# When conditioning tiles are loaded and multiplied in a hybrid decoder step: later loads, visits in pairs and triples, four tiles at the second norm

## The chip, the cores and the metric

One Trainium2 chip, one core. TensorE (PE) multiplies matrices into PSUM; VectorE (DVE), ScalarE (ACT) and GpSimd (POOL) do elementwise work; SyncE (SP) issues most of the DMA transfers from HBM into the on-chip SBUF. Each engine works through its own instructions in order, and engines wait for one another by semaphores. The metric is the device time of one execution in microseconds; a kernel's time is the median of its runs.

## The reference

One layer of a decoder, for a prompt (256 tokens) and eight samples of 4 tokens (288 token columns in all), D_MODEL 2048, float32:

```python
mod = jax.nn.silu(c) @ P['w_ada'] + P['b_ada']          # 9 conditioning rows, 2048 -> 6*2048
sh1, sc1, gt1, sh2, sc2, gt2 = [m[:, None, :] for m in jnp.split(mod, 6, axis=-1)]
xn = rmsnorm(x, P['g_norm1']) * (1.0 + sc1) + sh1
mix, st = mixer(xn, states[l], P)                       # RG-LRU, GLA and mLSTM branches, merged by gates
x = x + gt1 * mix
xn = rmsnorm(x, P['g_norm2']) * (1.0 + sc2) + sh2
x = x + gt2 * (jnp.square(jax.nn.relu(xn @ P['w_ff1'])) @ P['w_ff2'])
y = rmsnorm(x, g_final)
```

`mixer` multiplies `xn` by `w_in` (2048 x 12312), runs the three recurrent branches with their states, and merges them: `sum over branches of sigmoid(gate_b) * (y_b @ w_br_b)`, then `@ w_out`. All outputs, the new states too, are returned.

## The kernel before

**Layout.** Activations lie feature-major: 16 k-tiles of 128 features by 288 columns. SBUF holds ten large buffers (`slot(0)` to `slot(9)`, each 128 x 8 x 288), a ring buffer `ag` (one of 128 x 2048), two buffers `st` (128 x 1028; the states of GLA and mLSTM pass through them as well), and three buffers each for the weights' `raw`, `hi` and `lo`.

**Weight streams.** `stream` multiplies by a block of 512 output features. A step loads a 128 x 1024 weight tile (`raw`, L155, on SyncE's queue), rounds it to `hi` on ScalarE (L156), takes the rest `lo` on VectorE (L157), and does 24 matmuls of 288 columns: for four groups of features and two k-tiles hi x xh, hi x xl and lo x xh (L163 to L165). It yields after each step; `ahead` gives its loads and splits high priority.

**Conditioning.** `w_ada` is used by 16 k-rows for each of six vectors (SC1 in two halves of eight tiles, SH1, GT1, SH2, SC2, GT2 of sixteen tiles of 1024 KB each). `units()` lists them in the order in which they are needed, and after SH1 sixteen tiles of `win` for a correction (`cor`): the first three q/k/v blocks are multiplied before the shift SH1 is known, and SH1 times those weights is added at the end. `load_one` issues one tile's load (L264, L262 for `st`, where a tile is two halves, L270 for SC1, L276 for `cor`) into the next buffer of the list `slots["ids"]`; it waits in SyncE's queue until that buffer's earlier use is over. `visit` multiplies all loaded tiles on TensorE (L228) and, with the last of a vector, adds them up feature by feature (`by_feature` on VectorE, `ada_finish` or the correction's `finish`, L282 to L287). `drain(n)` loads and visits until n is done.

**Who comes when.** `every(p)` sets a pattern of letters, and `run` does one letter after each step of a stream: L loads a tile, V visits, X does both. `visit` is issued behind the last matmul of that step. SyncE is scheduled by hand, in the order of the program (`manual_schedule`); on the other engines a planner orders instructions by priority and by its own timeline.

**Stages.** SC1's first half is drained, `scale1(0)` scales k-tiles 0 to 7; three q/k/v blocks run over them (12 steps), then over k-tiles 8 to 15 (12 more), with pattern X. `shift` adds SH1: for four k-tiles at a time GpSimd adds xh + xl, VectorE and GpSimd add the shift, `split` makes new xh and xl. Then the fourth q/k/v block and two LRU blocks (24 steps, `cor`), the LRU, the gates, GLA, the merge of branch 0, the mLSTM with the merge of branch 1 filling in, the mLSTM's output gate `mo` (16 steps), the merge of branch 2 (48 steps; buffers 8 and 9 hold its input `yml`, buffer 5 the mLSTM's result `nT` before that), `wout` (32 steps), the second norm (`sumsq`, `rstd_of`, L1160 to L1166), and the MLP (`ff1`, `ff2`, 8 blocks).

Of the kernel before, what the change touches and what calls it, by code (L numbers as in the profile page):

```python
# [24 lines left out]
SH1, SC1, GT1, SH2, SC2, GT2 = range(6)  # L25
# [27 lines left out]
def trunk(ctx, tc, io):  # L53
    nc = tc.nc
    PSUM = bass.MemoryType.PSUM
    V, S, G, T, Q = nc.vector, nc.scalar, nc.gpsimd, nc.tensor, nc.sync
# [112 lines left out]
            yield  # L169


    pace = {"every": "", "n": 0, "last": None}

    def every(p):
        pace.update(every=p, n=0)

    def run(gen):
        for _ in gen:
            if pace["every"]:
                step(pace["every"][pace["n"] % len(pace["every"])])  # L180
                pace["n"] += 1


# [7 lines left out]
    mod = cp.tile([P, 6, KT, 9], F32, tag="mod", name="mod")  # L191
# [3 lines left out]
    def by_feature(ps, h, n):  # L195

        t = t288()[:, 0:n]
        V.transpose(t, ps[:, 256 * h:256 * h + n])
        return t.rearrange("p (m c) -> p m c", c=32)

    slots = {"ids": (None,), "n": 1}
# [11 lines left out]
    def cond_product(name, load, each, cols, stat, finish):  # L213


        acc_ = []

        def products(raw, q):
            if not acc_:
                acc_.append(pa.tile([P, 512], F32, tag="pa", name=nm("pa")))  # L220
            ps = acc_[0]
            w = cols // len(raw)
            for i in range(each):
                k = each * q + i
                for h, r in enumerate(raw):
                    v = r[:, w * i:w * i + w].rearrange("p (m j f) -> p j m f", j=4, f=32)
                    for j in range(4):
                        T.matmul(ps[32 * j:32 * j + 32, h * w // 4:(h + 1) * w // 4], stat(k), v[:, j], start=k == 0 and h == 0,  # L228
                                 stop=k == KT - 1, skip_group_check=True)

        def end():
            with tc.high_priority():
                for h in range(-(-cols // 1024)):
                    finish(h, by_feature(acc_[0], h, min(256, cols // 4 - 256 * h)))

        n = KT // each
        for q in range(n):
            def ld(q=q):
                raw = raw_tile()
                load(raw, q)  # L240
                return raw
            yield name, ld, lambda raw, q=q: products(raw, q), end if q == n - 1 else None
# [60 lines left out]
    def load_one():  # L303
        u = next(left, None)
        if u:
            held.append((u[0], u[1](), u[2], u[3]))

    def visit():

        while held:  # L310
            name, raw, products, end = held.pop(0)
            products(raw)
            if end:
                end()
                done.add(name)

    def step(c):
        if c in "LX":
            with tc.high_priority():
                load_one()  # L320
        if c in "VX":
            with tc.high_priority(), tc.issue_after(pace["last"].ins):
                visit()

    def drain(n):
        while n not in done:
            if not held:
                with tc.high_priority():
                    load_one()
            visit()  # L330


# [21 lines left out]
    def smp(a):  # L354
        return a[..., NP:N].rearrange("p k (b t) -> p k b t", b=NB)

    def modulate(xg, rs, k0, fk, xh, xl, xr):
# [3 lines left out]
        for j in range(0, 4, 2):  # L361
# [4 lines left out]
            G.tensor_tensor(out=xs, in0=xs, in1=mod[:, fk, r, 1:9].unsqueeze(3).to_broadcast(bc), op=ALU.mult)  # L366
            split(xh[:, r, :], xl[:, r, :], xr[:, j:j + 2])

    def shift(k0, shk, xh, xl, xr):

        h, l = xh[:, k0:k0 + 4, :], xl[:, k0:k0 + 4, :]
        G.tensor_tensor(out=xr, in0=h.bitcast(F32), in1=l.bitcast(F32), op=ALU.add)
        for i in range(4):
            V.tensor_scalar(xr[:, i, 0:NP], xr[:, i, 0:NP], mod[:, shk, k0 + i, 0:1], None, ALU.add)
        xs = smp(xr)
        G.tensor_tensor(out=xs, in0=xs, in1=mod[:, shk, k0:k0 + 4, 1:9].unsqueeze(3).to_broadcast([P, 4, NB, TS]), op=ALU.add)
        split(h, l, xr)

    def split(dst_h, dst_l, src):
        n = src.shape[1]  # L380
        step = 2 if len(src.shape) == 3 else n
        for a in range(0, n, step):
            r = slice(a, min(a + step, n))
            S.activation(dst_h[:, r], src[:, r], AF.Copy)  # L384
            V.tensor_tensor(out=dst_l[:, r], in0=src[:, r], in1=dst_h[:, r].bitcast(F32), op=ALU.subtract)  # L385
# [10 lines left out]
    xh = big.tile([P, KT, N], F32R, tag="xh", name="xh1")  # L396
# [24 lines left out]
    def plus_slot(dst, base):  # L421
        def f(m, p):
            V.tensor_tensor(out=dst[:, base + m, :], in0=dst[:, base + m, :], in1=p, op=ALU.add)
        return f
# [9 lines left out]
    scale1(0)  # L434
    G.tensor_copy(con[:, 0:1], mod[:, SC1, 0, 0:1])
    G.dma_start(con, io["con"])
    every("X")
    for b in range(NPRE):
        run(stream(win, B_Q + b, act1, 8, to_slot((qk, vv)[b // 2], 4 * (b % 2))))
    drain("sc")  # L440
    scale1(1)
    for b in range(NPRE):
        run(stream(win, B_Q + b, act1, KT, plus_slot((qk, vv)[b // 2], 4 * (b % 2)), k0=8))
    drain(SH1)
    for i in range(4):
        shift(4 * i, SH1, xh, xl, (xs3, xs4)[i % 2][:, 0:4, :])
    every("LLLL.V")
    slots.update(ids=(5, 6, 7, None, 0, 1, 3, 4), n=0)
    for b in range(NPRE, 4):
        run(stream(win, B_Q + b, act1, KT, to_slot((qk, vv)[b // 2], 4 * (b % 2))))  # L450
# [114 lines left out]
            V.scalar_tensor_tensor(sg[:, base + m, :], th, 1.0, p, ALU.add, ALU.mult)  # L565
        return f

    every("LLLL.V..")
    slots.update(ids=(6, 7, "st", None), n=0)
    run(stream(win, B_GATE, act1, KT, gate_silu(0)))  # L570
    run(stream(win, B_GATE + 1, act1, KT, gate_silu(4)))
# [225 lines left out]
    def merge(br, y, w):  # L797
        for b in range(4):
            if br == 0 and b == 2:
                visit()  # L800
                slots.update(ids=(None,), n=0)
                every("L.V...")
            if br == 0:
                gt = acc[b // 2][:, 4 * (b % 2):4 * (b % 2) + 4, :]
            elif br == 1:
                gt = ring.tile([P, 2048], F32, tag="ag", name=nm("ag"))[:, 0:4 * N].rearrange("p (k n) -> p k n", k=4)
            else:
                gt = slot(4)[:, 0:4, :]
            run(stream(win, B_MG + 4 * br + b, act1, KT, lambda m, p: S.activation(gt[:, m, :], p, AF.Tanh, scale=0.5)))

            def ev(m, p):
                k = 4 * b + m
                a = acc[k // 8][:, k % 8, :]
                if br == 0:
                    V.scalar_tensor_tensor(a, gt[:, m, :], 1.0, p, ALU.add, ALU.mult)
                    return
                t = t288()
                V.scalar_tensor_tensor(t, gt[:, m, :], 1.0, p, ALU.add, ALU.mult)  # L818
                G.tensor_tensor(out=a, in0=a, in1=t, op=ALU.add)  # L819
                if br == 2:  # L820
                    h, l = mrg[k // 8][:, k % 8, :], mrg[2 + k // 8][:, k % 8, :]
                    S.activation(h, a, AF.Copy, scale=0.5)
                    V.scalar_tensor_tensor(l, a, 0.5, h.bitcast(F32), ALU.mult, ALU.subtract)

            run(stream(w, b, lambda k: (y[0][:, k, :], y[1][:, k, :]), 8, ev))

    slots.update(ids=(None, 7), n=0)
    every("LL.V..")
    merge(0, ylru, io["wbl"])
    visit()  # L830
    every("")
# [254 lines left out]
    nT = mlstm()  # L1086

    merge(1, ygla, io["wbg"])

    mo = slot(3)  # L1090
    for b in range(2):
# [6 lines left out]
    yml = (slot(8, F32R), slot(9, F32R))  # L1098
    split(yml[0], yml[1], nT)

    slots.update(ids=(None, 5, "st"), n=0)
    every("LLL.V..")
    mrg.extend([slot(0, F32R), slot(1, F32R), slot(2, F32R), slot(3, F32R)])
    merge(2, yml, io["wbm"])


    visit()
    slots.update(ids=(8, 9, None, "st"), n=0)
    every("LLLL.V..LLL.V" + 20 * ".")
    x2 = (slot(4), slot(5))  # L1110
    for i in range(4):
        S.dma_start(x2[i // 2][:, 4 * (i % 2):4 * (i % 2) + 4, :], io["x"][:, 4 * i:4 * i + 4, :])
# [16 lines left out]
    def scaled(b):  # L1129

        x, f = (t[b // 2][:, 4 * (b % 2):4 * (b % 2) + 4, :] for t in (x2, xf))
        for i in range(4):
            G.tensor_scalar(f[:, i, 0:NP], x[:, i, 0:NP], mod[:, SC2, 4 * b + i, 0:1], None, ALU.mult)
        G.tensor_tensor(out=smp(f), in0=smp(x), in1=mod[:, SC2, 4 * b:4 * b + 4, 1:9].unsqueeze(3).to_broadcast([P, 4, NB, TS]), op=ALU.mult)

    for b in range(4):
        def ev_o(m, p, b=b):
            k = 4 * b + m
            x = x2[k // 8][:, k % 8, :]
            resid(x, p, GT1, k)  # L1140
            sumsq(pss, x, k, ssum)
            if k == KT - 4:
                S.activation(sc([P, 1], "warm", 1), ssum[:, 0:1], AF.Sqrt)
        if b == 3:
            drain(SC2)
            visit()
            every("")
            for i in range(3):
                scaled(i)
        run(stream(io["wout"], b, act_m, KT, ev_o))  # L1150
    scaled(3)
    rs = rstd_of(pss)
    xh2 = big.tile([P, KT, N], F32R, tag="xh", name="xh2")
# [50 lines left out]
    h = ff1(0)  # L1204
    at.update(raw=(None, None, 8))
    slots.update(ids=(9, None, "st"), n=0)
    every("L..L..L.." + "...V" + 8 * ".")
    for hb in range(8):
        hn = ff1(hb + 1) if hb < 7 else None
        if hb == 6:  # L1210
# [5 lines left out]
        h = hn  # L1216
# [120 lines left out]
```

## Time and profile before

| | us |
|---|---|
| runs | 2046.96, 2041.35, 2047.26 (median 2046.96) |
| profiled execution | 2053.96 |
| its span | 2052.2 |
| granted TensorE clock over the span | 0.984 |

In the profile an engine's row gives its busy time, its share of the span and its count of instructions; rows of a timeline give start and duration in us, engine, line, operation, output <- inputs, shape, and in brackets the idle time before it with what ended it. `xN` is a count (a float32 matmul counts twice). "SPq" is SyncE's queue: the row stands where a DMA is issued. A row of windows gives, after the stretch and its length, the busy time of PE, PEld (weight loads), DVE, ACT and POOL, then the granted clock, the DMA share and GB/s. A row of waits gives who waited for whom: total us, how often, the longest. A row of DMA issues ends in the KB of one and the median us from issue to landing.

### The profile page before, as it was taken

To read this page: it belongs to the slowest core of one execution; us is meant where nothing else is said; L and a number is where in the kernel's file an instruction comes from. 1 tells how busy PE (TensorE), PEld (TensorE's weight loads), DVE (VectorE), ACT (ScalarE), POOL (GpSimd) and SP (SyncE) were. 2 spreads that over 40 slices of the span, in tenths; PEclk is the share of its full clock that TensorE was granted. 3 is DMA by queue.
4 is the path that set the end of the run, shared out by engine and by line. 5 is a ranking of instruction groups with operands and counts; after the bars stand their busy time and mean duration, and the time that the engine had idled before them with its cause. 6 is when DMAs were issued, how large, how long until landed. Compare 5 with 4: busy or idle time off the path is not lost.

```text
span 2052.2 us, 35310 instructions
## 1 busy us (share of the span) xinstructions
PE 1970.7 (96%) x14846; PEld 1846.9 (90%) x14846; DVE 1029.1 (50%) x1422; ACT 801.6 (39%) x1103; POOL 309.2 (15%) x349
## 2 busy tenths in 40 slices
PE   6989999999899999989998999999999999999997
PEld 4769888998898988889988989999999999999997
DVE  4345566455672455544443564434444444444565
ACT  3323465232464322333333454434343434343433
POOL 0101213022321222100110441001010101010102
PEclk8999999999999999999999999999999999999999
DMA  9978756557442376657678446555655545445443
GB/s 376 387 279 288 291 197 236 194 183 275 143 156 92 124 251 211 222 206 277 260 258 302 155 134 234 209 181 207 222 195 181 183 154 174 166 154 176 164 156 116
DMA packets 119310, 429.48 MB, mean 209 GB/s; under 512 B 11744, under 2 KB 11904, under 8 KB 119024
## 3 DMA queue, kind: packets, MB, share of 16 engines
q1 hardware_dynamic: 110080, 393.59, 54.1%
q0 software_dynamic: 7920, 28.92, 3.9%
q10 hardware_dynamic: 1152, 4.72, 0.6%
q8 instruction: 116, 1.90, 0.4%
q14 instruction: 42, 0.34, 0.1%
HBM read 410.38 MB, written 16.81 MB: 208 GB/s over the span
## 4 chain that ended last, share of the span: by engine, by line
PE 86%; DMA 5%; DVE 4%; issue 3%; ACT 1%; POOL 1%; DVEq 0%; SPq 0%; ACTq 0%; POOLq 0%
PE mm L163 26%; PE mm L165 25%; PE mm L164 25%; PE pa L228 4%; DMA raw<-win 2%; DVE lo L157 1%; DMA st<-mC 1%; DMA raw<-wout 1%; DMA s<-wada 1%; ACT hi L156 1%; PE pi L1050 0%; PE px L1006 0%; DMA st<-gla 0%; PE px L723 0%; DVE s L465 0%
## 5 line engine op out<-in xcount | busy, mean ns | idle before, releaser
L157 DVE TENSOR_TENSOR lo<-raw,hi 128x1024 fp32r<-128x1024 f32 x450 | 576.2, 1284 | 629.9 <-ACT hi L156 619.1
L156 ACT ACTIVATE hi<-raw 128x1024 fp32r<-128x1024 f32 x450 | 476.3, 1060 | 847.2 <-PE mm L164 633.7
L163 PE MATMUL mm<-xh,hi 128*128 128x288 f32 x2576 | 767.0, 301 | 21.8 <-ACT xh L384 11.0
L164 PE MATMUL mm<-xl,hi 128*128 128x288 f32 x2576 | 763.1, 298 | 0.0
L165 PE MATMUL mm<-xh,lo 128*128 128x288 f32 x2576 | 742.3, 298 | 6.6 <-DVE lo L157 6.5
L163 PEld LDWEIGHTS mm<-xh,hi 128*128 128x128 f32 x2576 | 486.9, 189 | 53.0 <-issue 24.1
L163 PE MATMUL mm<-s,hi 128*128 128x288 f32 x1664 | 492.2, 298 | 7.6 <-ACT hi L156 7.6
L164 PEld LDWEIGHTS mm<-xl,hi 128*128 128x128 f32 x2576 | 488.5, 190 | 3.4 <-issue 1.5
L164 PE MATMUL mm<-s,hi 128*128 128x288 f32 x1664 | 490.7, 297 | 0.0
L165 PEld LDWEIGHTS mm<-xh,lo 128*128 128x128 f32 x2576 | 481.2, 190 | 10.1 <-DVE lo L157 7.9
L165 PE MATMUL mm<-s,lo 128*128 128x288 f32 x1664 | 477.5, 297 | 0.0
L163 PEld LDWEIGHTS mm<-s,hi 128*128 128x128 f32 x1664 | 314.3, 189 | 13.9 <-ACT hi L156 8.1
L164 PEld LDWEIGHTS mm<-s,hi 128*128 128x128 f32 x1664 | 314.7, 189 | 1.6 <-issue 1.2
L165 PEld LDWEIGHTS mm<-s,lo 128*128 128x128 f32 x1664 | 309.6, 189 | 1.3 <-issue 0.8
L1178 POOL TENSOR_TENSOR t<-t 128x288 f32<-128x288 f32 x64 | 60.4, 954 | 655.5 <-ACT t L1177 655.5
L157 DVE TENSOR_TENSOR lo<-s,hi 128x1024 fp32r<-128x1024 f32 x80 | 98.0, 1225 | 113.4 <-ACT hi L156 113.4
L156 ACT ACTIVATE hi<-s 128x1024 fp32r<-128x1024 f32 x80 | 84.9, 1061 | 140.4 <-PE mm L164 139.7
L819 POOL TENSOR_TENSOR s<-s,t 128x288 f32<-128x288 f32 x32 | 33.1, 1055 | 199.0 <-DVE t L818 198.9
L228 PE MATMUL pa<-s,silc 128*32 128x512 f32 (+1 forms) x512 | 54.8, 526 | 5.7 <-DMA s<-wada 5.7
L1194 DVE TENSOR_TENSOR s<-s,mm 128x288 f32<-128x288 f32 x96 | 40.4, 450 | 34.7 <-PE mm L165 33.6
L1059 DVE SCALAR_TENSOR_TENSOR st<-st,csb,px 128x257 f32<-128x257 f32 x64 | 28.6, 478 | 28.0 <-PE px L1058 20.2
L385 DVE TENSOR_TENSOR s<-t,s 128x288 fp32r<-128x288 f32 x64 | 33.9, 568 | 16.6 <-ACT s L384 16.6
(357 smaller groups left out, 1157.6 us busy)
## 6 DMA issues: line engine op xcount, KB each, us to landing
raw<-win SPq DMA_DIRECT2D x192, 512.0 KB, 4.8
raw<-wf SPq DMA_DIRECT2D x176, 512.0 KB, 4.3
s<-wada SPq DMA_DIRECT2D x51, 1024.0 KB, 8.2
s<-wf SPq DMA_DIRECT2D x80, 512.0 KB, 3.5
ag<-wada SPq DMA_DIRECT2D x30, 1024.0 KB, 6.9
raw<-wout SPq DMA_DIRECT2D x32, 512.0 KB, 4.2
st<-wada SPq DMA_DIRECT2D x30, 512.0 KB, 9.2
s<-win SPq DMA_DIRECT2D x14, 768.0 KB, 6.5
```

Source lines behind the costliest of these rows:

```text
L156: S.activation(hi, raw, AF.Copy)
L157: V.tensor_tensor(out=lo, in0=raw, in1=hi.bitcast(F32), op=ALU.subtract)
L163: T.matmul(pss[m][:, :N], hi[:, kk, ms], xh, start=k == k0, stop=False)
L164: T.matmul(pss[m][:, :N], hi[:, kk, ms], xl, start=False, stop=False)
L165: pace["last"] = T.matmul(pss[m][:, :N], lo[:, kk, ms], xh, start=False, stop=k == kt - 1)
L228: T.matmul(ps[32 * j:32 * j + 32, h * w // 4:(h + 1) * w // 4], stat(k), v[:, j], start=k == 0 and h == 0, stop=k == KT - 1, skip_group_ch ...
L385: V.tensor_tensor(out=dst_l[:, r], in0=src[:, r], in1=dst_h[:, r].bitcast(F32), op=ALU.subtract)
L819: G.tensor_tensor(out=a, in0=a, in1=t, op=ALU.add)
L1059: V.scalar_tensor_tensor(s4[:, i, d, :], s4[:, i, d, :], csb[:, h, b:b + 1], pu[:, 0:257], ALU.mult, ALU.add)
L1178: G.tensor_tensor(out=r, in0=r, in1=r, op=ALU.mult)
L1194: V.tensor_tensor(out=a, in0=a, in1=p, op=ALU.add)
```

## The change

The pattern becomes a list of words, each done after one step, with a number of steps to leave out first. New patterns: in the first stage four pairs, then triples and pairs in turn, and one last tile in step 21 of 24 (11 visits for the same 24 tiles); in `mo` four tiles from step 6 on, in the third merge 18 tiles from step 7 on (before 21 from step 1 on), in `wout` six tiles from step 7 on, and four more of GT2 that are multiplied behind its last step; the MLP keeps twelve. The buffer lists there are reordered. `load_one` loses its high priority; the correction's sums lose theirs, and both halves are transposed before either is added. `whole` does the additions xh + xl of all 16 k-tiles ahead of `drain(SH1)`, each into a place of its own; `shift` works two k-tiles at a time, the samples' sums on VectorE, with high priority.

```diff
-    def every(p):
-        pace.update(every=p, n=0)
+    def every(p, skip=0):
+
+        pace.update(every=p.split(), n=-skip)
...
         def end():
+            hs = range(-(-cols // 1024))
             with tc.high_priority():
-                for h in range(-(-cols // 1024)):
-                    finish(h, by_feature(acc_[0], h, min(256, cols // 4 - 256 * h)))
+                pvs = [by_feature(acc_[0], h, min(256, cols // 4 - 256 * h)) for h in hs]
+            for h in hs:
+                with tc.high_priority() if name != "cor" else nullcontext():
+                    finish(h, pvs[h])
...
-    def step(c):
-        if c in "LX":
-            with tc.high_priority():
+    def step(cs):
+        for c in cs:
+            if c == "L":
                 load_one()
-        if c in "VX":
-            with tc.high_priority(), tc.issue_after(pace["last"].ins):
-                visit()
+            elif c == "V":
+                with tc.high_priority(), tc.issue_after(pace["last"].ins):
+                    visit()
...
+    def whole(k0, xh, xl, xr):
+
+        G.tensor_tensor(out=xr, in0=xh[:, k0:k0 + 4, :].bitcast(F32), in1=xl[:, k0:k0 + 4, :].bitcast(F32), op=ALU.add)
+
     def shift(k0, shk, xh, xl, xr):
 
-        h, l = xh[:, k0:k0 + 4, :], xl[:, k0:k0 + 4, :]
-        G.tensor_tensor(out=xr, in0=h.bitcast(F32), in1=l.bitcast(F32), op=ALU.add)
-        for i in range(4):
-            V.tensor_scalar(xr[:, i, 0:NP], xr[:, i, 0:NP], mod[:, shk, k0 + i, 0:1], None, ALU.add)
-        xs = smp(xr)
-        G.tensor_tensor(out=xs, in0=xs, in1=mod[:, shk, k0:k0 + 4, 1:9].unsqueeze(3).to_broadcast([P, 4, NB, TS]), op=ALU.add)
-        split(h, l, xr)
+        for j in range(0, 4, 2):
+            r = slice(k0 + j, k0 + j + 2)
+            for i in range(j, j + 2):
+                V.tensor_scalar(xr[:, i, 0:NP], xr[:, i, 0:NP], mod[:, shk, k0 + i, 0:1], None, ALU.add)
+            xs = smp(xr[:, j:j + 2])
+            V.tensor_tensor(out=xs, in0=xs, in1=mod[:, shk, r, 1:9].unsqueeze(3).to_broadcast([P, 2, NB, TS]), op=ALU.add)
+            split(xh[:, r, :], xl[:, r, :], xr[:, j:j + 2])
...
-    every("X")
+    every("L LV " * 4 + "L LLV L LV " * 3 + "LV" + " ." * 40)
...
+    xrs = [(xs3, xs4)[i % 2][:, 4 * (i // 2):4 * (i // 2) + 4, :] for i in range(4)]
+    for i in range(4):
+        whole(4 * i, xh, xl, xrs[i])
     drain(SH1)
-    for i in range(4):
-        shift(4 * i, SH1, xh, xl, (xs3, xs4)[i % 2][:, 0:4, :])
-    every("LLLL.V")
+    with tc.high_priority():
+        for i in range(4):
+            shift(4 * i, SH1, xh, xl, xrs[i])
+    every("L L L L . V")
...
     merge(1, ygla, io["wbg"])
+    slots.update(ids=(None, "st"), n=0)
+    every("L L . V . . .", skip=5)
...
-    slots.update(ids=(None, 5, "st"), n=0)
-    every("LLL.V..")
+    visit()
+    slots.update(ids=(None, "st", 5), n=0)
+    every("L L L . V . .", skip=6)
     mrg.extend([slot(0, F32R), slot(1, F32R), slot(2, F32R), slot(3, F32R)])
     merge(2, yml, io["wbm"])
...
     visit()
-    slots.update(ids=(8, 9, None, "st"), n=0)
-    every("LLLL.V..LLL.V" + 20 * ".")
+    slots.update(ids=(None, "st", 8, 9), n=0)
+    every("L L L L . V . . L L . V . . L L L L" + 7 * " ." + " V", skip=6)
...
         if b == 3:
             drain(SC2)
-            visit()
-            every("")
             for i in range(3):
                 scaled(i)
         run(stream(io["wout"], b, act_m, KT, ev_o))
+    every("")
     scaled(3)
...
-    every("L..L..L.." + "...V" + 8 * ".")
+    every("L . . L . . L . . . . . V" + 7 * " .")
```

In the lists `None` is the ring buffer, `"st"` the pair of `st` buffers, a number a large buffer. `drain` loses its high priority too; the patterns that are not shown here keep their letters.

More of the change, by code (lines that the diff above doesn't have):

```diff
@@ L169, in stream @@
             yield
-    pace = {"every": "", "n": 0, "last": None}
-    def every(p):
-        pace.update(every=p, n=0)
+    pace = {"every": (), "n": 0, "last": None}
+    def every(p, skip=0):
+        pace.update(every=p.split(), n=-skip)
     def run(gen):
@@ L179, in run @@
             if pace["every"]:
-                step(pace["every"][pace["n"] % len(pace["every"])])
+                if pace["n"] >= 0:
+                    step(pace["every"][pace["n"] % len(pace["every"])])
                 pace["n"] += 1
@@ L327, in drain @@
             if not held:
-                with tc.high_priority():
-                    load_one()
+                load_one()
             visit()
@@ L566, in gate_silu @@
         return f
-    every("LLLL.V..")
+    every("L L L L . V . .")
     slots.update(ids=(6, 7, "st", None), n=0)
@@ L801, in merge @@
                 slots.update(ids=(None,), n=0)
-                every("L.V...")
+                every("L . V . . .")
             if br == 0:
@@ L827, in trunk @@
     slots.update(ids=(None, 7), n=0)
-    every("LL.V..")
+    every("L L . V . .")
     merge(0, ylru, io["wbl"])
```

## The prediction

> **What bounds the kernel now.** I read the page first, then the list of who made TensorE wait, then the stages by windows, then the timelines of TensorE and of SyncE around the long waits.
>
> ```profile
> span 2052.2 us, 35310 instructions
> PE 1970.7 (96%) x14846; PEld 1846.9 (90%) x14846; DVE 1029.1 (50%) x1422; ACT 801.6 (39%) x1103; POOL 309.2 (15%) x349
> 1650.00:1700.00 50.00, 50.00 (x378) 50.00 (x377) 23.91 (x28) 16.05 (x16) 0.00 (x0) 1.00 0.46 160
> PE mm L163 <- ACT hi L156: 14.2, 4, 6.2
> SPq L264 <- PE pa L228: 122.7, 30, 12.8
> SPq L264 <- DVE s L385: 16.1, 1, 16.1
> SPq L264 <- PE mm L165: 14.8, 9, 12.5
> ```
>
> TensorE is the bound: 96% busy. In the undisturbed window 378 matmuls take 50 us, 0.132 us each, so a stream step (24 matmuls) takes 3.17 us. All weight loads and all conditioning loads (L264) sit in one in-order queue, SyncE's. The last three rows show that queue standing still because a conditioning load's buffer is not free; the weight loads behind it come late, and that is what the longest row of TensorE's waits (for ScalarE's `hi`, which waits for a weight) ends in. A gain has two sources: fewer or cheaper TensorE instructions, or fewer stalls.
>
> **Part A, the first stage: 24 single visits become 11.** The cost of one visit is read from the timeline, that of several tiles at once from the chain.
>
> ```profile
> 83.25 1.06 PE L228 MATMUL pa<-s,silc 128*32 128x512 f32 x8
> 87.61 1.06 PE L228 MATMUL pa<-ag,silc 128*32 128x512 f32 x8
> 78.95 0.99 PE pa L228 x8
> 914.39 2.72 PE pa L228 x32
> 43.79 1.07 PE L228 MATMUL pa<-ag,silc 128*32 128x256 f32 x16
> 151.57 1.33 PE L163 MATMUL mm<-xh,hi 128*128 128x288 f32 x4 [6.16 <-ACT xh L384]
> 150.00:158.00 8.00, 6.40 (x33) 6.05 (x34) 7.02 (x6) 5.25 (x7) 3.55 (x2) 0.65 0.99 382
> ```
>
> From visit to visit 4.36 us pass; less 3.17 a visit costs 1.19. One tile takes 0.99 in the chain, three take 2.72: 0.865 a tile more, so each visit has a fixed part of 1.19 - 0.865 = 0.33. The tiles stay, 13 fixed parts go: 4.3 us. The old stage from the first visit's start: 23 x 3.17 + 24 x 1.195 = 101.6 from about 43.7, which gives 145.3; the row of the stall says 151.57 - 6.16 = 145.41. So the arithmetic holds, and the new stage ends at 43.7 + 72.9 + 24 x 0.865 + 11 x 0.33 = 141.
>
> The stall of 6.16 behind it has two causes, both touched. The shift (SH1) is only complete with the last step; by the new pattern the 24th tile is visited in step 21, so three steps (9.5 us) cover transposes, sums and the first k-tiles. And the queue was shut:
>
> ```profile
> 141.11 0.37 SPq L276 DMA_DIRECT2D s<-win  x1
> 141.57 0.44 SPq L155 DMA_DIRECT2D raw<-win  x1
> 149.89 1.06 ACT L156 ACTIVATE hi<-raw 128x1024 fp32r<-128x1024 f32 x1 [12.48 <-DMA raw<-win]
> ```
>
> The first load of the correction reuses a buffer visited two steps earlier, so it and the weight behind it went out at 141, and ScalarE stood at that weight until 149.89 with the shifted activations queued behind. In the new order that buffer was visited five steps earlier. I take the whole 6.16 away. The granted clock after the stall is 0.65 over 8 us, 2.8 us lost, of which 0.8 lie inside the stall: 2.0 more. Together 12.5. Against it: VectorE does the sums, two k-tiles a step, in the same three steps as weight splits; and loads now follow visits by three steps instead of five (DMA rival below). I set 1.5 against it: **A = 11**, ends 0 and 13. `whole` moves four GpSimd additions ahead of SH1, into time in which GpSimd idles, at nothing; if they came late the shift would be late by as much.
>
> The Trainium skill, TensorE: Matmul & The Clock Gate, Part 1, says that TensorE falls to half its clock after an idle window of about 3.4 us and needs as much work to come back; the 0.65 above agrees, and by that rule alone each removed stall would bring some 1.7 us beside its own length.
>
> **Part B, the correction's sums lose their priority.**
>
> ```profile
> 246.53 3.60 DVE L285 TENSOR_SCALAR s<-s,cor 128x256 f32<-128x256 f32 x8
> 256.38 1.21 DVE L157 TENSOR_TENSOR lo<-raw,hi 128x1024 fp32r<-128x1024 f32 x1
> 257.65 0.40 PE L165 MATMUL mm<-xh,lo 128*128 128x288 f32 x1 [3.78 <-DVE lo L157]
> ```
>
> TensorE waits 3.78 for a `lo` behind these sums and the convolution (L465). Without priority they may go behind it; but the convolution stays ahead, and VectorE is handed the same work. **B = 1**, ends -2 and 5.
>
> **Part C, tiles in the mLSTM's output gate (mo), and the third merge.** What goes:
>
> ```profile
> 879.04 0.33 SPq L155 DMA_DIRECT2D raw<-win  x1
> 895.98 0.46 SPq L155 DMA_DIRECT2D raw<-win  x1
> 903.01 0.61 PE L163 MATMUL mm<-xh,hi 128*128 128x288 f32 x1 [5.18 <-ACT hi L156]
> 902.00:912.00 10.00, 8.99 (x56) 8.99 (x57) 4.90 (x4) 4.71 (x5) 0.00 (x0) 0.77 0.81 293
> ```
>
> The queue stands 16 us at slot 5 (nT), and TensorE 5.18. The new order comes to slot 5 only in step 9 of the merge. Gain 5.18, and of the 2.3 us that the clock's 0.77 over 10 us means, 1.7 behind the stall.
>
> What comes: four tiles in mo, first load in step 6 (ring), second in step 7: the two `st` buffers. These belong to the mLSTM's states until the last two are stored:
>
> ```profile
> 844.30 0.53 POOL L1060 DMA_DIRECT2D o_C_s<-st  x1 [1.02 <-DVE st L1059]
> 851.29 0.54 POOL L1046 DMA_DIRECT2D st<-mC  x1 [6.46 <-DMA o_C_s<-st]
> 861.25 0.53 POOL L1060 DMA_DIRECT2D o_C_s<-st  x1 [6.95 <-DVE st L1059]
> 858.67 0.40 ACT L1093 ACTIVATE s<-mm 128x288 f32<-128x288 f32 x1
> 868.72 1.16 PE L583 MATMUL pi<-s,ones 128*32 128x288 f32 x10
> raw<-win SPq DMA_DIRECT2D x192, 512.0 KB, 4.8
> ```
>
> A buffer comes free some 7 us after its store is issued (844.30 to 851.29). The last store goes out at 861.25, or 1.6 earlier with no stream work between, so the second `st` load waits until about 866.5, and step 8's weight behind it with it: 4.8 us to land, 1.06 for ScalarE's `hi` (row at 149.89), first matmul near 872. Before, the first six matmuls of step 8 were read out at 858.67, so the step began near 857.8. Of these 14 us the states' own small products (the sums over heads, 1.16 in the row, and a few like it) fill an estimated 3.5: a new stall of 10.5 and 1.7 of clock, 12. Visits: seven in the merge become two in mo and six, for the tiles that wout gives up, so no more in all. **C = 6.9 - 12 = -5**, ends -16 and +7: if SyncE gets the `st` buffers ahead of the last states, nothing stalls; if it gets one, the states run on one buffer.
>
> **Part D, wout.**
>
> ```profile
> 1059.09 0.33 SPq L155 DMA_DIRECT2D raw<-wout  x1
> 1071.95 0.38 SPq L264 DMA_DIRECT2D s<-wada  x1
> 1072.43 0.41 SPq L155 DMA_DIRECT2D raw<-wout  x1
> 1095.28 0.40 PE L163 MATMUL mm<-s,hi 128*128 128x288 f32 x1 [1.41 <-ACT hi L156]
> 1080.00:1090.00 10.00, 8.68 (x44) 8.68 (x45) 2.45 (x2) 3.06 (x3) 0.00 (x0) 0.63 1.03 418
> ```
>
> The same at slot 8, which the third merge reads to its end: 12.9 us of a shut queue, the longest stall of the list (6.2), another of 1.41, and 3.7 of clock in the window, of which 1 lies in the stall. By the new order slot 8 is asked for in step 9, and every reuse lies three steps or more behind its visit. **D = 6.2 + 1.4 + 2.7 = 10**, ends 3 and 11.
>
> **Part E, four tiles at the second norm.**
>
> ```profile
> 1191.78 0.75 PE L343 MATMUL pi<-t,ones 128*128 128x288 f32 x2
> 1194.95 0.75 PE L343 MATMUL pi<-t,ones 128*128 128x288 f32 x2 [0.47 <-ACT t L339]
> 1199.90 0.44 PE L163 MATMUL mm<-xh,hi 128*128 128x288 f32 x1 [4.20 <-DVE xl L1165]
> ```
>
> The MLP stage loses four tiles and two of its six visits: 4 x 0.865 + 2 x 0.33 = 4.1, all on TensorE's path. They go to the stretch 1191.7 to 1199.9, in which TensorE has little but the sums of squares. If they run wholly ahead of these sums, rstd is late by up to 2.5; between and behind them, by nothing. **E = 4.1 - 0.5 = 3.6**, ends 1 and 6 (6 if the shorter gap keeps the clock up, worth 2 as in A).
>
> **Sum.** 11 + 1 - 5 + 10 + 3.6 = 20.6. The profiled run took 2053.96 (span 2052.2), 7 above the median of 2046.96; taken from the median: **2026**.
>
> **Rivals.** (1) *No new stall in mo*: the `st` buffers come in time, C = +7. For it: who gets a free buffer is the planner's choice, which no row shows. 12 more: 2014. (2) *One of the two buffers is taken early*, the states go on with one and the second load waits for the last of them, 11.5 later: C = -16, 2037. (3) *The first stage becomes DMA-bound, and the kernel slower.* Reuse three steps behind a visit leaves 3 x 3.17 + 2.07 - 2.3 = 9.3 us for the next weight to land:
>
> ```profile
> 50.00:60.00 10.00, 10.00 (x91) 8.50 (x91) 2.92 (x3) 4.52 (x7) 0.00 (x0) 1.00 1.02 414
> raw<-win SPq DMA_DIRECT2D x27, 512.0 KB, 8.2
> ```
>
> The second row is the median of that stage, 28 to 150 us: 1.1 us of margin, at a DMA share of 1.02. There are six such places; from a landing time of about 13 us on they cost 6 x 4 = 24 and eat the whole gain, and at 14 the kernel takes 2052. Against it: 24 tiles of 1.05 MB and 24 weights of 0.52 MB are 37.8 MB, 91 us at 414 GB/s, done by 122 from 31 on, while TensorE asks for the last tile at 130. The Trainium skill, DMA: Bandwidth & Descriptors, Bandwidth, holds some 358 GB/s for what one core gets from HBM; by that the last tile would land at 137 and this rival would begin to bite, an estimate of 6 us; the measured 414 decides against it. (4) *The waits move*: with the queue open the next in line ends the stalls (VectorE's shift, the merge's last sums, another planner's order around the states), half the gain of A and D goes: 2038.
>
> **How the numbers follow.** Forecast 0.42, 2026 (its own range 2017 to 2035); (1) 0.22, 2014; (2) 0.07, 2037; (3) 0.11, 2045 to 2060; (4) 0.18, 2030 to 2048. What a measurement of this kernel can tell is about 0.3%, 6 us: faster below 2041, slower above 2053. Faster: 0.42 + 0.21 + 0.05 + 0.02 + 0.09, with a cut for planner's surprises, 0.78; same 0.12; slower 0.10. The range 2007 to 2045 leaves out 0.2, nearly all of it above.
>
> **What would show it.** A: the visits from 44 to 132 come in pairs and triples with 2.72 for a triple, the B_Q+3 stream starts near 141 without a wait above 1 us. C: no wait of 5 at the merge's third step, but one of 10 in mo after the last state product, its weight issued behind an `st` load. D: no wait of SyncE for L165. E: L228 between 1191 and 1200 of the old time, and four visits after it. Wrong would be: stalls of TensorE for a conditioning tile in the first stage (3), or no stall in mo (1).

## The result and the profile after

| | us |
|---|---|
| before, median of four runs beside it | 2047.11 |
| after: 2027.16, 2029.36, 2027.14, 2029.23 | median 2028.2 |
| ratio, with its 95% interval | 0.9915 [0.9896, 0.9933] |
| profiled execution after, its span, granted clock | 2027.16, 2025.4, 0.987 |

The change makes the kernel 18.9 us faster. The two profiled spans lie further apart, 26.8 us, since the profiled execution of before was 7 above its median.

The head of the page of the changed kernel, the first rows of the list of TensorE's waits, and three of SyncE's:

```profile
span 2025.4 us, 35339 instructions
PE 1961.3 (97%) x14862; PEld 1843.7 (91%) x14862; DVE 1027.3 (51%) x1430; ACT 800.3 (40%) x1103; POOL 306.3 (15%) x345
```
```profile
PE pi L1062 <- DMA st<-mC: 6.5, 5, 2.5
...
PE mm L163 <- ACT hi L156: 4.4, 2, 3.0
PE mm L163 <- DVE xl L1179: 4.2, 1, 4.2
```
```profile
SPq L269 <- PE pa L230: 155.3, 28, 12.8
...
SPq L267 <- DMA o_C_s<-st: 24.6, 2, 19.7
```

(The new lines: L228 became L230, the loads L264 and L262 became L269 and L267, L384 became L392, the sums of squares L343 became L347, and `xl` ahead of the MLP L1165 became L1179.) The row that led the list, TensorE for a `hi` that waits for its weight, fell from 14.2 to 4.4. SyncE's wait at slot 5 for VectorE (16.1) is gone, and its waits for stream matmuls fell from 14.8 (longest 12.5) to 2.7 (longest 0.6). Its waits for earlier visits rose from 122.7 to 155.3 while the kernel got faster: what costs time is a weight behind such a wait that comes late, and the sum of the row does not tell that. One row is new: SyncE stands 19.7 us at a load into `st`, whose buffer is still being stored as mLSTM state.

The first stage, the place where its stall stood, and the mLSTM's output gate, in TensorE's timeline:

```profile
47.69 1.07 PE L230 MATMUL pa<-ag,silc 128*32 128x256 f32 x16
...
131.39 1.06 PE L230 MATMUL pa<-s,silc 128*32 128x512 f32 x8
144.38 0.37 PE L163 MATMUL mm<-xh,hi 128*128 128x288 f32 x1 [2.19 <-DVE s L431]
...
247.32 0.61 PE L165 MATMUL mm<-xh,lo 128*128 128x288 f32 x1 [3.77 <-DVE lo L157]
...
845.03 1.21 PE L127 MATMUL px<-row,con 128*128 128x288 f32 x4 [3.28 <-DVE row L602]
849.21 0.61 PE L163 MATMUL mm<-xh,hi 128*128 128x288 f32 x1 [2.96 <-ACT hi L156]
```

The last tile of the first stage is multiplied at 131.4, and the next stage starts at 144.38 instead of 151.57. The gap for `lo` ends at 247.32 instead of 257.65: 10.3 earlier. The start of step 8 of `mo` stood near 857.8 and now stands at 849.2, only 8.6 earlier, although one weight before it the lead had been 18.5 (the seventh weight's `hi` at 825.7 instead of 844.2). That is the new stall. How it comes about, in the timelines of SyncE, GpSimd and ScalarE:

```profile
817.53 0.33 SPq L155 DMA_DIRECT2D raw<-win  x1
837.73 0.33 SPq L267 DMA_DIRECT2D st<-wada  x1
843.21 0.33 SPq L267 DMA_DIRECT2D st<-wada  x1
843.63 10.90 SPq L155 DMA_DIRECT2D raw<-win  x6
```
```profile
834.36 0.53 POOL L1072 DMA_DIRECT2D o_C_s<-st  x1 [3.90 <-DVE st L1071]
838.91 0.53 POOL L1072 DMA_DIRECT2D o_C_s<-st  x1 [4.02 <-DVE st L1071]
```
```profile
848.10 1.06 ACT L156 ACTIVATE hi<-raw 128x1024 fp32r<-128x1024 f32 x1 [5.20 <-DMA raw<-win]
```

Between 817.5 and 843.6 SyncE issues no weight. The two `st` loads (837.73 and 843.21) wait for the two last stores (834.36 and 838.91); step 8's weight goes out behind them, lands, is rounded at 848.10, and TensorE goes on at 849.2.

The stretch at the second norm (TensorE, then ScalarE):

```profile
1164.53 1.92 PE L230 MATMUL pa<-s,silc 128*32 128x512 f32 x16
1166.27 1.04 PE L230 MATMUL pa<-ag,silc 128*32 128x512 f32 x8
1167.13 0.61 PE L230 MATMUL pa<-st,silc 128*32 128x256 f32 x6
1167.67 0.75 PE L347 MATMUL pi<-t,ones 128*128 128x288 f32 x2
1168.84 0.63 PE L230 MATMUL pa<-st,silc 128*32 128x256 f32 x6
...
1170.57 0.63 PE L230 MATMUL pa<-st,silc 128*32 128x256 f32 x4
1171.12 0.75 PE L347 MATMUL pi<-t,ones 128*128 128x288 f32 x2
1176.08 1.33 PE L163 MATMUL mm<-xh,hi 128*128 128x288 f32 x4 [4.20 <-DVE xl L1179]
```
```profile
1171.91 0.50 ACT L354 ACTIVATE row<-pi,eps 128x288 f32<-128x288 f32 x1 [4.21 <-PE pi L347]
```

Three tiles and part of the fourth (16 + 8 + 6 matmuls) stand ahead of the first sum, six more matmuls of it behind that sum, and its last four still ahead of the last one (1171.12). The gap ahead of the MLP is 4.20, just what it was before: the tiles pushed the whole chain (sums, rstd, scaling, MLP) back instead of filling the gap in it.

### The profile page after: what moved, and what is told of

Its sections match the earlier page's. It is cut to its first block, busy times and chain, and to the rows that moved or that the text cites. A ratio compares the mean times of both kernels' runs of the same rounds, so it can differ in the third digit from the quotient of the medians.

```text
span 2025.4 us, 35339 instructions
## 1 busy us (share of the span) xinstructions
PE 1961.3 (97%) x14862; PEld 1843.7 (91%) x14862; DVE 1027.3 (51%) x1430; ACT 800.3 (40%) x1103; POOL 306.3 (15%) x345
## 4 chain that ended last, share of the span: by engine, by line
PE 89%; DMA 4%; DVE 3%; issue 2%; POOL 1%; ACT 1%; DVEq 0%; ACTq 0%; SPq 0%; POOLq 0%
PE mm L163 27%; PE mm L165 26%; PE mm L164 26%; PE pa L230 4%; DMA s<-wada 1%; DVE lo L157 1%; DMA st<-mC 1%; DMA s<-x 0%; DMA o_C_s<-st 0%; PE px L1018 0%; PE pi L1062 0%; PE px L735 0%; DVE s L477 0%; PE px L626 0%; POOL lho L561 0%
## 5 line engine op out<-in xcount | busy, mean ns | idle before, releaser
L230 PE MATMUL pa<-s,silc 128*32 128x512 f32 (+1 forms) x488 | 49.3, 514 | 5.4 <-DMA s<-wada 5.4
L1071 DVE SCALAR_TENSOR_TENSOR st<-st,csb,px 128x257 f32<-128x257 f32 x64 | 28.5, 479 | 27.2 <-PE px L1070 18.0
```

The costliest lines, as they stand in the source:

```text
L1071: V.scalar_tensor_tensor(s4[:, i, d, :], s4[:, i, d, :], csb[:, h, b:b + 1], pu[:, 0:257], ALU.mult, ALU.add)
```

## The experiments

Below, "time" is the median, with the ratio to the kernel before and its interval. The medians of before in the three groups of runs that follow were 2046.66, 2046.65 and 2047.28, so the groups can be held against each other. "In place" is a difference read between two traces at one place. For the norm two lengths are used: from the end of wout's last matmul to the MLP's first one (norm), and from there to TensorE's last instruction (MLP).

**How much two executions of one kernel differ.** Both kernels were run again, unedited.

> The changed kernel once more, as the yardstick for the others of this group. Accounting of the prediction: about 19 us under the kernel before in the medians (2028 against 2047). If the trace of before was an unlucky one (its run was 7 above the median), its waits for the mLSTM's states and not the changed queue explain part of the 26.8 us between the two spans; then this trace shows waits for st<-mC that differ by several us from the 6.5 of the first trace of the changed kernel.

> The kernel before once more, for its trace. If the waits for the mLSTM's states (st<-mC 9.7 us) and for the GLA's (3.8) in the first trace are typical, they come again within 2 us each and the changed kernel's smaller ones (6.5 and 0.4) are an effect of the change; if not, they are chance, and the span is nearer to 2045 than to 2052.

After: 2027.05, 0.9911 [0.9891, 0.993], span 2024.0. Before: 2050.04 in one run, span 2048.2. The stalls stand at the same places, most of them within half a microsecond in length; the wait for step 8's `hi` in `mo` is 1.6 instead of 3.0. What differs more are TensorE's waits for the states of mLSTM and GLA. The first fence is the execution of before that the prediction was read from, the second the new one:

```profile
PE pi L1050 <- DMA st<-mC: 9.7, 5, 3.8
...
PE pi L760 <- DMA st<-gla: 3.8, 1, 3.8
```
```profile
PE pi L1050 <- DMA st<-mC: 7.8, 4, 3.4
...
PE pi L760 <- DMA st<-gla: 1.5, 3, 0.6
```

The sum falls from 13.5 to 9.3, by 4.2, and the span by 4.0. In the two executions of after the same rows sum to 6.9 and 5.1. So a good part of the 9 us by which after gains between 300 and 825 us in the two first traces is the lot of one execution; in the second pair of traces it is 3.9. The other runs say how wide such a lot is. From the `lo` gap to the seventh weight's `hi` in `mo` before took 586.5 and 581.0 us, after 578.4 and 577.1, and the ten variants of after that follow between 575.7 (c_early) and 586.1 (best1). No effect of the change can be told from that spread, and two single traces can't be compared across this stretch to better than some us.

**The first stage: one tile at a time again (a_single).**

```diff
-    every("L LV " * 4 + "L LLV L LV " * 3 + "LV" + " ." * 40)
+    every("LV " * 24)
```

> The changed kernel with 24 single visits in the first stage, one after each step; the shift stays in its new form. Theory: 13 more visits at 0.33 us are 4.3, SH1 is complete with the last step and the first load of the correction shuts the queue, a stall of about 6 as before and 2 of clock: 9 to 13 us slower than the changed kernel. Rival (the new shift by itself, with its sums ahead, took away the stall): only the visits, 3 to 5 us slower.

Time 2040.65, 0.9969 [0.9957, 0.9982]: 12 to 14 us above after. The old stall is back, on ScalarE that waits for its weight 12.1 us:

```profile
151.65 1.33 PE L163 MATMUL mm<-xh,hi 128*128 128x288 f32 x4 [5.81 <-ACT xh L392]
...
259.09 0.61 PE L165 MATMUL mm<-xh,lo 128*128 128x288 f32 x1 [3.77 <-DVE lo L157]
```
```profile
149.97 1.06 ACT L156 ACTIVATE hi<-raw 128x1024 fp32r<-128x1024 f32 x1 [12.13 <-DMA raw<-win]
```

By the end of the `lo` gap it is 11.8 behind after (259.09 against 247.32). With the new shift in place, the grouping carries the whole gain of the stage: without it the new shift brings nothing (the `lo` gap ended at 257.65 before the change).

**Which of the two causes of the stall (a_lead).** Single visits as above, but the buffers in another order, so that the correction's first loads go to buffers that have long been free: the queue stays open, the shift stays late.

```diff
-    slots.update(ids=(5, 6, 7, None, 0, 1, 3, 4), n=0)
+    slots.update(ids=(0, 1, 5, 6, 7, None, 3, 4), n=0)
```

> The changed kernel with 24 single visits, as in a_single, but the correction's first loads go to buffers 0 and 1, which have been free for a dozen steps, so that the queue stays open at the end of the stage. Theory (two causes at the stall: the shut queue and the shift that is complete only with the last step): TensorE's wait at the start of the fourth block falls from 5.8 to some 2 to 4 (sums, rounding and the first k-tiles), the kernel is 2 to 4 us faster than a_single (2040.7), about 2037. Rival A (the queue alone made the stall): the wait goes below 1, 6 to 8 us faster than a_single. Rival B (the shift alone): the wait stays at 5 or more, no faster.

Time 2040.48, 0.9973 [0.9956, 0.999]: no faster than a_single. TensorE, VectorE and ScalarE:

```profile
148.15 1.33 PE L163 MATMUL mm<-xh,hi 128*128 128x288 f32 x4 [3.12 <-ACT xh L392]
153.14 0.61 PE L164 MATMUL mm<-xl,hi 128*128 128x288 f32 x1 [3.66 <-DVE xl L393]
```
```profile
146.27 0.34 DVE L252 TENSOR_TENSOR mod<-t,par 128x72 f32<-128x72 f32 x2
146.57 0.62 DVE L382 TENSOR_SCALAR s<-s,mod 128x256 f32<-128x256 f32 x2
...
152.34 0.75 DVE L393 TENSOR_TENSOR xl<-s,xh 128x576 fp32r<-128x576 f32 x1
```
```profile
140.02 1.06 ACT L156 ACTIVATE hi<-raw 128x1024 fp32r<-128x1024 f32 x1 [3.08 <-DMA raw<-win]
```

The queue was open indeed: the weight was rounded at 140.0, 10 us earlier than in a_single. But SH1 was complete only at 146.6, and VectorE then ran nearly all the sums of the shift before it made the first `xl`. The waits of 5.8 and 1.0 in a_single became 3.1 and 3.7, the same in sum; by the `lo` gap 1.2 us were gained (257.86 against 259.09). I had expected 2 to 4. So the shift that comes late holds the stall even with the queue open. The reverse, an early shift with the queue shut, was not run. In a_single ScalarE rounded the weight at 149.97 and made the first `xh` right behind it, so the shut queue may hold nearly as much by itself.

**Pairs and triples, but the old shift (a_oldshift).** The functions `whole` and `shift` as before, in the order of before, without high priority; the new pattern stays.

```diff
-    for i in range(4):
-        whole(4 * i, xh, xl, xrs[i])
     drain(SH1)
-    with tc.high_priority():
-        for i in range(4):
-            shift(4 * i, SH1, xh, xl, xrs[i])
+    for i in range(4):
+        shift(4 * i, SH1, xh, xl, (xs3, xs4)[i % 2][:, 0:4, :])
```

> The changed kernel with its pairs and triples, but the shift as before: four k-tiles at a time, the sums xh + xl after SH1 and in two shared places, samples on GpSimd, no high priority. Theory (what matters is that SH1 is complete three steps earlier): within 2 us of the changed kernel (2028). Rival (the four sums of 3.5 us on GpSimd behind SH1, and their places in turn, hold up the fourth block): a new wait of TensorE between 140 and 165, 3 to 8 us slower.

Time 2032.21, 0.993 [0.9909, 0.995], 4 to 5 above after in the medians, with intervals that overlap. In place 2.3 (the `lo` gap ends at 249.66 against 247.32), from two short waits:

```profile
143.81 0.40 PE L163 MATMUL mm<-xh,hi 128*128 128x288 f32 x1 [1.71 <-DVE s L427]
...
147.31 0.40 PE L165 MATMUL mm<-xh,lo 128*128 128x288 f32 x1 [2.17 <-DVE lo L157]
```

In place that is near the 2 us of the theory; the second wait is new, as the rival had it, but short. Of the stage's gain some 8 come from the earlier SH1 and the fewer visits, about 2 from the shift in its new form, together with the grouping.

**The stop at `st` (c_slot8).** In `mo` the second buffer is slot 8, which is free there, instead of the pair `st`.

```diff
-    slots.update(ids=(None, "st"), n=0)
+    slots.update(ids=(None, 8), n=0)
```

> The changed kernel, but the four tiles in mo go to the ring and to large buffer 8 (free between the second and the third merge) and not to the ring and the two st buffers. Theory (the queue stands behind the st load until the mLSTM's last states are stored): the stop of SyncE of 19.7 us for o_C_s goes, the three waits of TensorE between 839 and 849 (0.8, 3.3, 3.0) go or move, and the kernel is 7 to 12 us faster than the changed one. Rival (TensorE waits there for the mLSTM's own last chain, the queue is only seen beside it): SyncE's stop goes too, but the waits stay and the time is within 3 us.

Time 2017.96, 0.9857 [0.9844, 0.9871]: 9 to 10 below after, and the intervals do not touch. SyncE's weights go on through the stretch in which they stood still, and TensorE works through it at full clock:

```profile
839.68 0.33 SPq L155 DMA_DIRECT2D raw<-win  x1
...
848.66 0.41 SPq L155 DMA_DIRECT2D raw<-win  x1
```
```profile
830.00:850.00 20.00, 19.20 (x146) 15.83 (x145) 9.57 (x14) 6.96 (x11) 1.07 (x2) 1.00 0.60 192
```

In after the stretch from 840 to 860 reads thus:

```profile
840.00:860.00 20.00, 13.73 (x84) 11.31 (x88) 13.19 (x18) 10.27 (x15) 0.00 (x0) 0.83 0.61 218
```

**Who gets the `st` buffers first (h_prio).** `load_one` with its high priority again; all else as in after.

```diff
             if c == "L":
-                load_one()
+                with tc.high_priority():
+                    load_one()
```

> The changed kernel with load_one at high priority again, in the steps and in drain. Theory (SyncE's order is the program's, so priority only says who gets a free st buffer): where the st load in mo now gets its buffers ahead of the last states, SyncE's stop for o_C_s of 20 us gets shorter or goes, and the states come later; between 8 us faster and 5 us slower than the changed kernel. Rival (priority of a load on a queue in program order does nothing): within 1.5 us, SyncE's stop still 19 to 21 us.

Time 2031.66, 0.9921 [0.9901, 0.9941], 3 to 5 above after in the medians, with intervals that overlap. The row of SyncE's wait is the old one:

```profile
SPq L267 <- DMA o_C_s<-st: 26.1, 2, 20.6
```

The priority of the load does not decide who gets `st`; both ways the states keep both buffers until their last stores, and the load waits. That is the rival's sign, but its 1.5 us are not met in the medians, and what makes the rest is open.

**The third merge's first buffers (c_early).** On top of c_slot8, the third merge loads from its first step on and comes to slot 5 in step 2, as before.

```diff
-    slots.update(ids=(None, "st", 5), n=0)
-    every("L L L . V . .", skip=6)
+    slots.update(ids=(None, 5, "st"), n=0)
+    every("L L L . V . . " * 6 + ". " * 6)
```

> c_slot8 (2018.0), but the third merge's loads begin in its first step and use buffer 5 second, as before the change; the last six steps load nothing, so the counts stay. Theory (shut queue at nT): SyncE stops for nT's split, TensorE waits about 5 us for a weight in the merge's third step; 5 to 8 us slower than c_slot8. Rival (that wait came from the mLSTM's end, which is the same here): under 2 us.

Time 2026.52, 0.9897 [0.9877, 0.9918], 8.6 above c_slot8 (beside the runs of before in its own group: 2047.28 against 2046.66). In place it is less:

```profile
880.43 0.40 PE L163 MATMUL mm<-xh,hi 128*128 128x288 f32 x1 [3.10 <-ACT hi L156]
```

SyncE stands 4 us at slot 5, TensorE 3.1, and at the start of the MLP the two traces are 3.4 apart (1172.2 against 1168.8). The direction is as expected, the size of 5 to 8 is not borne out in place, and what makes the rest of the medians' distance I can't say; its runs spread over 9 us (2022.2 to 2031.6), and the profiled one was the fastest of the six.

**wout's first buffers (d_early).** wout loads from its first step on, slots 8 and 9 first.

```diff
-    slots.update(ids=(None, "st", 8, 9), n=0)
-    every("L L L L . V . . L L . V . . L L L L" + 7 * " ." + " V", skip=6)
+    slots.update(ids=(8, 9, None, "st"), n=0)
+    every("L L L L . V . . L L . V . . . . . . . . L L L L" + 7 * " ." + " V")
```

> The changed kernel with wout's loads as before the change: from its first step on and to buffers 8 and 9 first, which the third merge still reads. Theory (shut queue): SyncE stops some 12 us for the end of the merge, TensorE waits some 6 us for its second or third weight of wout and runs at half clock behind it; 8 to 11 us slower than the changed kernel. Rival (the wait at wout had to do with the load of the DMA engines, x and four tiles at once): the same stop of SyncE but under 3 us.

Time 2040.54, 0.997 [0.9957, 0.9982]: 12 to 14 above after, where 8 to 11 were expected; in place 11.3, from step 8 of `mo` (850.73 against 849.21) to wout's end (1177.41 against 1164.60). SyncE's stop and both old gaps are back, so the rival (under 3 us) fails:

```profile
SPq L269 <- PE mm L165: 15.7, 4, 14.3
```
```profile
1067.60 0.61 PE L163 MATMUL mm<-s,hi 128*128 128x288 f32 x1 [5.69 <-ACT hi L156]
...
1077.94 0.40 PE L163 MATMUL mm<-s,hi 128*128 128x288 f32 x1 [1.23 <-ACT hi L156]
```

**The four tiles behind the sums instead of ahead of them (n_late).** The visit at wout's last step is left out and issued behind the last sum of squares.

```diff
-    every("L L L L . V . . L L . V . . L L L L" + 7 * " ." + " V", skip=6)
+    every("L L L L . V . . L L . V . . L L L L" + 8 * " .", skip=6)
...
-            T.matmul(ps[:, :N], ones, sq, start=k == KT - 4, stop=k == KT - 1)
+            pace["sum"] = T.matmul(ps[:, :N], ones, sq, start=k == KT - 4, stop=k == KT - 1)
...
     rs = rstd_of(pss)
+    with tc.high_priority(), tc.issue_after(pace["sum"].ins):
+        visit()
```

> The changed kernel, but the four tiles at the second norm are multiplied behind the last sum of squares and not behind wout's last step. Theory (the tiles ran ahead of the sums and held up rstd by 3.4 us): the last sum ends some 4 us after wout's last matmul as before the change (not 7.5), TensorE's wait of 4.2 us shrinks below 1.5, and the kernel is 3 to 5 us faster than the changed one. Rival (the tiles cost their time wherever they stand, since the norm's chain needs VectorE and not TensorE): within 1.5 us.

Time 2024.43, 0.9892 [0.9876, 0.9908]: 2.6 and 3.8 below the two medians of after, where 3 to 5 were expected, and the intervals overlap. In place the gain is larger and plain:

```profile
1172.03 0.75 PE L347 MATMUL pi<-t,ones 128*128 128x288 f32 x2 [0.46 <-ACT t L343]
1172.72 1.92 PE L230 MATMUL pa<-s,silc 128*32 128x512 f32 x16
...
1175.32 1.05 PE L230 MATMUL pa<-st,silc 128*32 128x256 f32 x16
1176.99 0.79 PE L163 MATMUL mm<-xh,hi 128*128 128x288 f32 x4 [0.63 <-DVE xl L1181]
```

The same four tiles now stand in the old gap, of which 0.63 is left. The norm takes 8.12 instead of 11.48, and the MLP 833.09 instead of 835.41. The second gain is the clock: 10 us at 0.75 instead of 1.00 are 2.5. The MLP's first 10 us, in after and in n_late:

```profile
1176.08:1186.08 10.00, 10.00 (x58) 10.00 (x59) 8.72 (x20) 6.34 (x18) 5.82 (x15) 0.75 0.06 10
```
```profile
1177.00:1187.00 10.00, 10.00 (x75) 10.00 (x76) 8.43 (x18) 5.69 (x16) 5.20 (x12) 1.00 0.19 58
```

**No tiles at the norm (n_mlp16).** The four go back to the MLP, which has its sixteen again.

```diff
-    every("L L L L . V . . L L . V . . L L L L" + 7 * " ." + " V", skip=6)
+    every("L L L L . V . . L L . V" + 14 * " .", skip=6)
```

> The changed kernel without the four tiles at the second norm: the MLP stage keeps all sixteen, in six visits. The prediction's term E: 3.6 us slower than the changed kernel. By the trace of the changed kernel (the norm later by 3.4 us, the MLP stage shorter by 3.0): within 1.5 us.

Time 2030.77, 0.9926 [0.9912, 0.9941], 2.6 and 3.7 above the two medians of after. That looks like the 3.6 of the prediction, and it isn't:

| | norm | MLP | sum |
|---|---|---|---|
| before | 8.11 | 838.76 | 846.87 |
| n_mlp16 | 8.11 | 838.62 | 846.73 |
| after | 11.48 | 835.41 | 846.89 |
| n_late | 8.12 | 833.09 | 841.21 |

From wout's end on, after and n_mlp16 take the same time; the difference lies ahead of it. In these two traces wout ends at 1164.60 in after and at 1167.98 in n_mlp16. Half of the 3.4 us is there when the third merge starts (884.94 against 886.67), and n_mlp16 shows a gap of 1.4 near 957 that after lacks. Why, I have not tested.

**The two repairs together (best1).** c_slot8 and n_late.

> Both repairs together: mo's tiles to buffer 8, the norm's tiles behind the sums. If both theories hold and add: 10 to 16 us faster than the changed kernel, about 2014. If the stalls only move: within 4 us of the better of the two.

Time 2013.14, 0.9834 [0.9818, 0.985]: faster than both kernels, 14 to 15 below after and some 33 below before. It is 4.8 below c_slot8, a second sign of what n_late gains; the norm takes 8.1 and the MLP 833.1, as in n_late.

## Why the prediction was right, and where not

The forecast of 2026 came within 2.2 us of the measured 2028.2, and the direction rests on the mechanism that was argued: SyncE's queue, shut by conditioning loads that wait for their buffers, and too many visits. Term by term:

**A, forecast 11.** 10.3 in place, 11.8 by a_single. The parts were sized less well than their sum. The last tile is multiplied at 131.4, where TensorE was to ask for it at 130, with no wait of TensorE for a tile from 44 to 132 at 405 GB/s between 100 and 120 us, so rival (3), the DMA-bound stage, did not come. But the stage ended at 142.2 and not at 141 (3.2 us gained by the visits, not 4.3), and the next began at 144.4, with a wait of 2.2 where none above 1 was forecast:

```profile
142.00:150.00 8.00, 5.81 (x44) 5.65 (x43) 8.00 (x17) 2.32 (x3) 0.00 (x0) 1.00 0.81 309
```

VectorE has no idle moment in these 8 us: the shift's sums and splits, the weights' `lo` and the read-out of the previous blocks (L431) share it. The 1.5 set against the gain stood for this and came out larger. The visits and the shorter wait make 7.2 in place, and the other 3.1 come by the `lo` gap, where 2.0 were reckoned for the clock (1.00 here). Of the stall's "two causes" the late shift is shown to hold it without the other: a_lead opened the queue alone and gained 1.2. Whether the shut queue would hold it too is not shown. For the DMA rate the Trainium skill, HBM Reference, Specifications (TRN2), tells of about 425 GB/s for a core that streams alone, against 358 as a core's share when both cores of a pair do; the measured 405 over 20 us, in a program on one core, lies above the second and below the first, so the 358 that the prediction weighed was not the figure for this case. Two prices of the rivals are 2 us off by the prediction's own terms: six places at 14 - 9.3 = 4.7 are 28, so 2054 and not 2052 in (3), and half of A and D is 10.5, so 2036.5 and not 2038 in (4).

**B, forecast 1.** Nothing: the gap is 3.78 before and 3.77 after. The step that failed is "Without priority they may go behind it". VectorE's order around the gap is the same in both traces: the transposes, the sums and the convolution in turn, and only then the `lo`. A likely reason stands in the code: the correction's `end` runs within `visit`, and `step` wraps `visit` in high priority, so leaving out the inner one need not take anything away. No run takes away the outer one, so this stays an argument.

**C, forecast -5.** The gain at the merge came (no stall at its third step), the new stall too: 9 to 10 by c_slot8 instead of 12. Overstated was its length. A buffer was reckoned free 7 us after its last store was issued; here the loads went out 3.4 and 4.3 after theirs (834.36 to 837.73, 838.91 to 843.21). And the one wait of 10 came as three, 0.82, 3.28 and 2.96, with the states' products between them. Rival (1) fell by the same run, and h_prio showed that its lever, the load's priority, doesn't move the buffers.

**D, forecast 10.** Confirmed: both gaps gone, and back with d_early, which is 12 to 14 slower. The two terms at the merge and wout together, 6.9 + 10 = 16.9, are 18.6 in place (the lead grows from 8.6 at 849 to 27.2 at wout's end). By c_early the merge's part is the less certain: 3.4 in place, 8.6 in the medians, where the prediction had 6.9.

**E, forecast 3.6.** Zero in place: the MLP won 3.35, the norm lost 3.37. The MLP's gain was to be 4.1; its first 10 us ran at a granted clock of 0.75 instead of 0.83 before, and 10 x 0.08 are 0.8 of what is missing. The term that failed is the 0.5 for the delay of rstd. The planner set all four ahead of the last sum, three of them and more ahead of the first, and the chain was held up by 3.4; the 2.5 given as the most was too low, since four tiles alone are 4 x 0.865 = 3.46. The row quoted there, a gap of 4.20 that ends in `xl`, says that TensorE's idle time lies behind rstd, so only work that is ordered behind the sums can fill it; n_late does that and gains 5.7 in place.

**The sum.** In place the terms make -10.3 (A), about +9.9 (mo), -18.6 (merge and wout) and 0 (norm and MLP): -19.0, beside the 18.9 of the medians. A, B and E gave 5.3 too little; C and D, forecast at 5 together, gave 8.7 (the lead grows from 18.5 to 27.2) and made up 3.7 of it: the closeness is partly luck. How the 8.7 split depends on where `mo` is cut off: two steps later, at step 10, the lead is only 6.3 (864.90 against 858.57, counted at 24 matmuls a step), and before still has work on the states to do there. In the second pair of traces A brings 10.4, C and D 10.0 and E 0.4, 20.8 together. The other 8 of the two profiled spans' 26.8 lie in the stages of the states, where the waits for the states of GLA and mLSTM make 6.6 of them (13.5 against 6.9).

## What to carry over

Where one in-order queue issues both what is needed soon and what can wait, look at each load's buffer: a load that comes before its buffer is free stops everything behind it, and a free buffer (c_slot8) or a later place in the order (the reverse of d_early, which changes the buffers too) is worth about 10 us at two places here; at the third, in the merge, c_early gives 3 to 9. When two causes lie under one stall, remove them one at a time before crediting either: the open queue alone gained 1.2, and only with the earlier shift as well did most of the stall go. And work given to an engine's gap fills it only if it is ordered behind the instruction that the gap's other end depends on; ahead of it, it moves the gap.

## What was not expected of the hardware

The stretch behind a gap of 4.20 us runs at a granted clock of 0.75 for 10 us, and with only 0.63 idle at 1.00, and the MLP is 2.3 us shorter. The Trainium skill, TensorE: Matmul & The Clock Gate, Part 1, lets the clock fall after an idle window of about 3.4 us that isn't tied to the instructions; that fits, as does the execution of before, which with the same gap of 4.20 shows 0.83 in its first 10 us. The length of one gap doesn't tell all: in after, behind two waits of 3.28 and 2.96 with 1.21 us of products between them, the granted clock was 0.64 from 849.2 to 855.2, and behind the single wait of 2.19 it was 1.00. The waits for the states of GLA and mLSTM, 13.5 and 9.3 us in two executions of the same kernel, were the other surprise: a difference of 4 us between two traces in those stages means nothing.
